# Second layer's value product turned round: activations stationary, value rows moving, sums kept in PSUM over all blocks

## The chip, the core and the metric

The kernel runs on one core of a Trainium2 chip. The metric is the device time of one execution in microseconds (us). A change of about 0.5% (20 us) is what the measurement of this kernel can tell from none.

## The reference

Two layers of a backbone over 512 latent tokens (width 1024) with 256 context tokens. Each layer has a token mixer and then PEER, a retrieval over 16384 experts, of which each token picks 128 (8 heads, 16 each). The part that matters here:

```python
def peer(h, wq, keys, u_tab, v_tab):
    ...                                                  # scores, two top-k, softmax
    def run(args):
        xc, ec, gc = args                                # tokens, experts, gates
        a = jax.nn.gelu(jnp.einsum('tkd,td->tk', u_tab[ec], xc))
        return jnp.einsum('tk,tkd->td', a * gc, v_tab[ec])
...
        if last:
            xl = xl + g2 * peer(hl, peer_wq[i], peer_keys[i], peer_u[i], peer_v[i])
...
    return rmsnorm(xl, final_g)
```

## The kernel before

**Layout.** The latent stream `x_l` stands feature-major: 128 partitions by 8 feature blocks by 512 tokens. Matrix products run in two parts: each fp32 operand is split into a rounded `hi` and a rest `lo` (float32r), and three matmuls (hi hi, hi lo, lo hi) make one product. `load_split` (lines 158 to 165) loads 512 KB of weights on SP's queue into a raw buffer, ACT rounds it (`whi`, L163), VectorE subtracts (`wlo`, L164).

**PEER in the second layer** (`peer`, from line 807). 384 of the 512 tokens (`TD`, three token tiles, `td`) are computed densely over all 128 blocks of 128 experts: an up-projection per block (`u_phase`, L822 to L829, matmuls in `proj` at L315 to L317, gelu by ACT at L825), a multiply with the dense gates `gt` (L999), a split into `ahi` and `alo` (L1004, L1005), and the value product. The last 128 tokens are gathered: GpSimd fetches the 128 rows of u and then of v that each token picked (L834, 512 KB each), and VectorE takes the dot products (`u_job`, L839) and the weighted sum (`v_job`, L850). At the end of `v_job` the sum is transposed back and added to `x_l` (L858, L862).

**Stages.** 62 of the 128 up-projections (`AHEAD`) are done early, while gates are being built, and spilled to HBM (`ad`); 66 are done inside the value stage (`prep` calls `u_phase`). All loads, and the gathered rows too, share one ring of nine raw buffers (`raw_tile`, 6 + 3). `pace` hands out the remaining gather jobs over the value stage: two steps for each up-projection, one for each value load.

**The value stage** (L1014 to L1034). It runs over 16 groups of eight expert blocks (`GS`). At a group's head all eight blocks are prepared (two of them already at the end of the group before, `EXC`); then, for each of the eight feature blocks `db`, one load of value weights, 24 matmuls with the value weights stationary and 384 tokens moving (L1020 to L1022), summed over the group's blocks in a PSUM tile `sc`, and one VectorE update of `x_l` from it (L1023). After the last group come the sums of squares (`stat`), `rsqrt`, a broadcast over TensorE (L252), eight scalings (L1042) and eight output transfers.

**Order.** The Tile framework orders each engine's instructions by a simulated timeline and generates the waits; each engine works through its list in order. PSUM has three tags with two buffers each: `mm` (one bank each), `sc` (two banks each) and `tp` (one bank each), eight banks in all.

## Time and profile before

| | us |
|---|---|
| median of 3 runs | 4072.15 (4067.31 to 4084.64) |
| profiled execution, its own time | 4055.16 |
| its span in the trace | 4053.4 |
| mean granted clock of TensorE over the span | 0.955 of 2.4 GHz |

The profile is that of one execution. Lines such as L1023 are lines of the kernel before. PE is TensorE, PEld its weight loads, DVE VectorE, ACT ScalarE, POOL GpSimd, SP the engine that issues most loads; SPq is its queue. PE's busy time includes the end of each matmul, which the next one overlaps, so starts are the better measure.

### The profile page before, as it was taken

How to read it: one execution, taken by the hardware profiler on the slowest of the kernel's cores; microseconds unless marked ns; L12 is line 12 of the kernel's file. 1: busy time of each engine (PE TensorE's matmuls, PEld its weight loads, DVE VectorE, ACT ScalarE, POOL GpSimd, SP SyncE). 2: the span in 40 equal slices, each digit the busy share in tenths (PEclk: the TensorE clock that was granted, in tenths of full speed). 3: DMA queues.
4: the chain of work that ended last, by engine and by line, in shares of the span. 5: the costliest groups of instructions: out<-in, count | busy, mean ns of one | idle time of the engine just before them, and what ended most of it. 6: DMA issues, size and time to landing. Idle time of an engine off the chain costs nothing. (4 is left out here: it accounts for less than half of the span.)

```text
span 4053.4 us, 54311 instructions
## 1 busy us (share of the span) xinstructions
PE 3695.2 (91%) x19469; PEld 3153.8 (78%) x19469; DVE 3273.7 (81%) x6850; ACT 1482.4 (37%) x2113; POOL 1050.3 (26%) x783
## 2 busy tenths in 40 slices
PE   7989889999978898999989988989999999998988
PEld 4777768877866777777768767779998888888887
DVE  8955799998997787788979885479998777777776
ACT  4344433224663222222322334433485332332322
POOL 0000000243324443455545300000003333333331
PEclk9989889999989999999999998999999999999998
DMA  7601135588989998999989662034579988888974
GB/s 247 224 31 44 52 111 168 185 311 301 338 308 315 309 315 295 316 327 327 334 303 339 235 226 79 1 120 130 164 283 340 313 291 284 281 280 278 310 267 157
DMA packets 378136, 966.64 MB, mean 238 GB/s; under 512 B 30712, under 2 KB 160552, under 8 KB 370312
## 3 DMA queue, kind: packets, MB, share of 16 engines
q1 hardware_dynamic: 239480, 467.60, 34.5%
q0 software_dynamic: 111312, 406.29, 29.2%
q10 hardware_dynamic: 27072, 89.27, 5.6%
q8 instruction: 153, 2.51, 0.2%
q14 instruction: 119, 0.97, 0.1%
HBM read 871.68 MB, written 91.36 MB: 238 GB/s over the span
## 5 line engine op out<-in xcount | busy, mean ns | idle before, releaser
L163 ACT ACTIVATE whi<-raw 128x1024 fp32r<-128x1024 f32 x640 | 672.6, 1057 | 1524.0 <-PE sc L1021 651.0
L834 POOL DMA_INDIRECT raw<-in_u_n_dram,E x384 | 499.3, 1300 | 2287.8 <-DVE wlo L164 1049.7
L315 PE MATMUL mm<-hi_l,whi 128*128 128x512 f32 (+1 forms) x2656 | 995.7, 375 | 18.7 <-ACT a L825 8.6
L317 PE MATMUL mm<-hi_l,wlo 128*128 128x512 f32 (+1 forms) x2656 | 989.0, 372 | 10.6 <-DVE wlo L164 10.6
L316 PE MATMUL mm<-lo_l,whi 128*128 128x512 f32 (+1 forms) x2656 | 990.3, 373 | 4.5 <-DVE lo_l L295 4.3
L1020 PE MATMUL sc<-ahi,whi 128*128 128x512 f32 (+1 forms) x2048 | 752.7, 374 | 82.7 <-DVE x_l L1023 69.3
L164 DVE TENSOR_TENSOR wlo<-raw,whi 128x1024 fp32r<-128x1024 f32 x640 | 776.4, 1217 | 62.3 <-ACT whi L163 54.2
L1021 PE MATMUL sc<-alo,whi 128*128 128x512 f32 (+1 forms) x2048 | 768.3, 376 | 60.4 <-DVE alo L1005 59.2
L1022 PE MATMUL sc<-ahi,wlo 128*128 128x512 f32 (+1 forms) x2048 | 760.3, 372 | 15.3 <-DVE wlo L164 15.2
L834 POOL DMA_INDIRECT raw<-in_v_n_dram,E x384 | 544.7, 1419 | 641.7 <-DVE ht L850 326.3
L839 DVE SCALAR_TENSOR_TENSOR raw<-raw,ht 128x1024 f32<-128x1024 f32 x384 | 466.6, 1221 | 170.9 <-DMA raw<-in_u_n_dram,E 169.3
L850 DVE SCALAR_TENSOR_TENSOR ht<-raw,wg,ht 128x1024 f32<-128x1024 f32 x381 | 487.8, 1280 | 129.9 <-DMA raw<-in_v_n_dram,E 127.5
L315 PEld LDWEIGHTS mm<-hi_l,whi 128*128 128x128 f32 x2656 | 502.9, 189 | 90.1 <-ACT a L825 11.1
L317 PEld LDWEIGHTS mm<-hi_l,wlo 128*128 128x128 f32 x2656 | 502.6, 189 | 81.1 <-DVE wlo L164 17.8
L316 PEld LDWEIGHTS mm<-lo_l,whi 128*128 128x128 f32 x2656 | 503.3, 189 | 73.9 <-DVE lo_l L295 9.2
L1020 PEld LDWEIGHTS sc<-ahi,whi 128*128 128x128 f32 x2048 | 395.6, 194 | 146.4 <-DVE x_l L1023 51.0
L1021 PEld LDWEIGHTS sc<-alo,whi 128*128 128x128 f32 x2048 | 397.9, 194 | 127.2 <-DVE alo L1005 87.6
L1022 PEld LDWEIGHTS sc<-ahi,wlo 128*128 128x128 f32 x2048 | 398.3, 194 | 59.4 <-DVE wlo L164 19.2
L1004 ACT ACTIVATE ahi<-a 128x512 fp32r<-128x512 f32 (+1 forms) x256 | 146.2, 577 | 543.9 <-DVE a L999 540.1
L958 ACT ACTIVATE gs<-sc 128x1024 f32<-128x1024 f32 x112 | 213.9, 2017 | 64.7 <-PE sc L956 61.0
L999 DVE TENSOR_TENSOR a<-a,gt 128x512 f32<-128x512 f32 (+1 forms) x256 | 156.1, 619 | 88.6 <-DMA gt<-gd 64.5
L1023 DVE SCALAR_TENSOR_TENSOR x_l<-sc,mods,x_l 128x512 f32<-128x512 f32 (+1 forms) x256 | 171.6, 679 | 68.0 <-PE sc L1022 65.8
(287 smaller groups left out, 3782.0 us busy)
## 6 DMA issues: line engine op xcount, KB each, us to landing
raw<-in_u_t_dram SPq DMA_DIRECT2D x256, 512.0 KB
raw<-in_v_b_dram SPq DMA_DIRECT2D x256, 512.0 KB
gd<-gs ACTq DMA_DIRECT2D x56, 1024.0 KB
raw<-in_w_adt_dram SPq DMA_DIRECT2D x64, 512.0 KB
gt<-gd SPq DMA_DIRECT2D x15, 2048.0 KB
raw<-in_wq_dram SPq DMA_DIRECT2D x48, 512.0 KB
gt<-gd SPq DMA_DIRECT2D x15, 1536.0 KB
ad<-a ACTq DMA_DIRECT2D x70, 256.0 KB
```

What stands on the lines that cost most here:

```text
L163: nc.scalar.activation(hi, raw, AF.Copy)
L164: nc.vector.tensor_tensor(lo, raw, hi.bitcast(F32), op=ALU.subtract)
L315: nc.tensor.matmul(ps, whi[:, k], hhi[:, k], start=(k == 0), stop=False)
L316: nc.tensor.matmul(ps, whi[:, k], hlo[:, k], start=False, stop=False)
L317: nc.tensor.matmul(ps, wlo[:, k], hhi[:, k], start=False, stop=(k == K - 1))
L834: nc.gpsimd.indirect_dma_start(out=g, out_offset=None, in_=tab, in_offset=bass.IndirectOffsetOnAxis(ap=G["E"][:, it, k:k + 1], axis=0), el ...
L839: nc.vector.scalar_tensor_tensor(g, g, 1.0, G["ht", it], op0=ALU.mult, op1=ALU.mult, accum_out=G["dots", it][:, k:k + 1])
L850: nc.vector.scalar_tensor_tensor(G["acc", it], g, G["wg", it][:, k:k + 1], G["acc", it], op0=ALU.mult, op1=ALU.add)
L958: nc.scalar.activation(gs[:, :, t8:t8 + 8].rearrange("p i t -> p t i"), ps, AF.Copy, scale=1.0 / WSC)
L1020: nc.tensor.matmul(ps, vh[:, c], wh, start=(c == 0), stop=False)
L1021: nc.tensor.matmul(ps, vh[:, c], wl, start=False, stop=False)
L1022: nc.tensor.matmul(ps, vl[:, c], wh, start=False, stop=(c == GS - 1))
```

## The change

In the second layer alone (`last`), the value product is turned round. For each expert block the activations of a token tile (128 experts by 128 tokens, `ahi` and `alo`) are stationary, and 128 natural value rows (128 experts by 1024 features, in two halves of 512) move: 18 matmuls of 512 columns for a block. The token-major sums of the three token tiles stay in six PSUM banks (both `sc` and both `tp` buffers) over all 128 blocks. Blocks are prepared two ahead instead of a group at a time, and the gates of a group (`gt`) are loaded one group ahead into a second buffer. A new `fin_setup` transposes `x_l` to token-major (`xt`) and spreads the gate `g2` over partitions at the head of the stage; a new `fin` adds gate times sum, norms and writes a token tile, for the gathered tile when its last row has come, for the three others after the last block. The final block after the two layers goes. The output and `final_g` are laid out token-major by the host code.

```diff
-    fg = const("final_g", [P, K])
...
             jobs = []
+            tok = {}
+
...
-                if k == P - 1:
+                if k == P - 1 and last:
+                    tok["fin"](td + it, [G["acc", it]])
+                elif k == P - 1:
                     xd, ms, ct = G["dst", it]
...
+            def fin_setup(pools):
+                fp = pools.enter_context(tc.tile_pool(name=nm("fin"), bufs=1))
+                xt = fp.tile([P, NL, D], F32, name=nm("x_tok"))
+                g2 = fp.tile([P, D], F32, name=nm("g2row"))
+                for hf in range(2):
+                    sl = slice(hf * 512, (hf + 1) * 512)
+                    pb = ps_mm()
+                    for k in range(4):
+                        nc.tensor.matmul(pb[:, k * P:(k + 1) * P], mcol(l, G2, 4 * hf + k, 0).to_broadcast([P, P]), ident,
+                                         start=True, stop=True)
+                    nc.scalar.activation(g2[:, sl], pb, AF.Copy)
+                for t in range(NL):
+                    for hf in range(2):
+                        pb = ps_mm()
+                        for k in range(4):
+                            nc.tensor.transpose(pb[:, k * P:(k + 1) * P], x_l[:, 4 * hf + k, t * P:(t + 1) * P], ident)
+                        nc.scalar.activation(xt[:, t, hf * 512:(hf + 1) * 512], pb, AF.Copy)
+
+                def fin(t, parts):
+                    w = D // len(parts)
+                    y = T(fp, [P, D], F32, "y", bufs=1)
+                    for j, ps in enumerate(parts):
+                        sl = slice(j * w, (j + 1) * w)
+                        nc.vector.tensor_tensor(y[:, sl], ps, g2[:, sl], op=ALU.mult)
+                        nc.vector.tensor_tensor(xt[:, t, sl], xt[:, t, sl], y[:, sl], op=ALU.add)
+                    ss = T(tiny, [P, 1], F32, "f_ss")
+                    nc.scalar.activation(y, xt[:, t], AF.Square, accum_out=ss)
+                    rstd = T(tiny, [P, 1], F32, "f_rs")
+                    rsqrt(rstd, ss, 1.0 / D, 1)
+                    nc.vector.scalar_tensor_tensor(xt[:, t], xt[:, t], rstd, fgr, op0=ALU.mult, op1=ALU.mult)
+                    nc.sync.dma_start(out[:, t], xt[:, t])
+
+                fgr = fp.tile([P, D], F32, name=nm("fgr"))
+                nc.sync.dma_start(fgr, a["final_g"])
+                tok["fin"] = fin
+
...
-                vps = [es2.enter_context(tc.tile_pool(name=nm("vp"), bufs=4))]
+                vps = [] if last else [es2.enter_context(tc.tile_pool(name=nm("vp"), bufs=4))]
...
-                vps.insert(0, es2.enter_context(tc.tile_pool(name=nm("vp"), bufs=6)))
+                vps.insert(0, es2.enter_context(tc.tile_pool(name=nm("vp"), bufs=4 if last else 6)))
+                gtps = [gtp]
+                if last:
+                    gtps.append(es2.enter_context(tc.tile_pool(name=nm("gtq"), bufs=1)))
+                    fin_setup(es2)
...
+                gts = {0: gt}
+
+                def load_gt(g):
+                    if 0 < g < ng and g not in gts:
+                        gts[g] = gt_tile(gtps[g % len(gtps)])
+                        nc.sync.dma_start(gts[g], gv[:, :TD // GT, g * GS:(g + 1) * GS, :])
 
                 def prep(g, c):
-                    nonlocal gt
-                    if g and c == 0:
-                        gt = gt_tile()
-                        nc.sync.dma_start(gt[:, :TD // GT], gv[:, :TD // GT, g * GS:(g + 1) * GS, :])
+                    load_gt(g)
+                    if last and c == 1:
+                        load_gt(g + 1)
+                    gt = gts[g]
...
-                for g in range(ng):
+                if last:
+                    halves = [slice(0, 512), slice(512, D)]
+                    acc2 = [ps_sc(), ps_sc()]
+                    accs = [[x[:, h] for h in halves] for x in acc2] + [[ps_tp(), ps_tp()]]
+                    prep(0, 0)
+                    prep(0, 1)
+                    for i in range(NKEYS):
+                        if i + 2 < NKEYS:
+                            prep(*divmod(i + 2, GS))
+                        wh, wl = ready.pop(divmod(i, GS))
+                        vh, vl = load_split(a["v_n"][e0 + i * P:e0 + (i + 1) * P], (P, D))
+                        for t in range(td):
+                            sl = slice(t * P, (t + 1) * P)
+                            for j, (w, v) in enumerate(((wh, vh), (wh, vl), (wl, vh))):
+                                for h in range(2):
+                                    nc.tensor.matmul(accs[t][h], w[:, sl], v[:, halves[h]], start=(i == 0 and j == 0),
+                                                     stop=(i == NKEYS - 1 and j == 2))
+                            if i == NKEYS - 1:
+                                tok["fin"](t, accs[t])
+                        pace(1)
+
+                for g in range(0 if last else ng):
...
-    o = T(hpool, [P, K, L], F32, "hi_l")
-    rb = rows(st_l)
-    for k in range(K):
-        nc.vector.scalar_tensor_tensor(o[:, k], x_l[:, k], fg[:, k:k + 1], rb, op0=ALU.mult, op1=ALU.mult)
-        nc.sync.dma_start(out[:, k], o[:, k])
```

## Rows read from the trace of the kernel before

**Rows 1.** The page: busy time of two engines (share of the span, instructions), and what the transfers moved in each of 40 equal slices of the span.

```profile
PE 3695.2 (91%) x19469; PEld 3153.8 (78%) x19469; DVE 3273.7 (81%) x6850; ACT 1482.4 (37%) x2113; POOL 1050.3 (26%) x783
...
GB/s 247 224 31 44 52 111 168 185 311 301 338 308 315 309 315 295 316 327 327 334 303 339 235 226 79 1 120 130 164 283 340 313 291 284 281 280 278 310 267 157
```

**Rows 2.** Two stretches, the value stage of the second layer and that of the first: length, then busy us of PE, PEld, DVE, ACT and POOL (instructions), granted clock, busy share of the DMA engines, GB/s.

```profile
3122.00:4037.00 915.00, 831.76 (x4498) 805.95 (x4498) 694.71 (x934) 278.00 (x382) 299.89 (x237) 0.95 0.83 277
1238.00:2342.00 1104.00, 1027.61 (x4391) 826.99 (x4390) 914.34 (x1118) 297.60 (x383) 526.55 (x377) 0.98 0.88 307
```

**Rows 3.** Timeline of TensorE in the second layer's value stage, 384 columns moving: start, us, what. 26 matmuls lie between the two.

```profile
4012.07 0.33 PE L1020 MATMUL sc<-ahi,whi 128*128 128x384 f32 x1
...
4016.75 0.33 PE L1020 MATMUL sc<-ahi,whi 128*128 128x384 f32 x1
```

**Rows 4.** The same in the first layer's value stage, 512 columns moving. 22 matmuls lie between the two.

```profile
2200.54 0.39 PE L1020 MATMUL sc<-ahi,whi 128*128 128x512 f32 x1
...
2205.75 0.39 PE L1022 MATMUL sc<-ahi,wlo 128*128 128x512 f32 x1
```

**Rows 5.** Groups of instructions in 3122 to 4037 us: line, engine, operation, tiles, shapes, count, busy us, mean ns of one, idle us before them and what ended it. L1020 to L1022 are alike, and L315 to L317.

```profile
L1021 PE MATMUL sc<-alo,whi 128*128 128x384 f32 x1008 | 354.1, 352 | 33.2 <-DVE alo L1005 33.2
L164 DVE TENSOR_TENSOR wlo<-raw,whi 128x1024 fp32r<-128x1024 f32 x186 | 225.3, 1218 | 7.5 <-ACT whi L163 6.7 <-issue 0.3 <-DMA raw<-in_v_b_dram 0.3
L163 ACT ACTIVATE whi<-raw 128x1024 fp32r<-128x1024 f32 x185 | 193.6, 1056 | 392.6 <-PE sc L1021 275.1 <-PE mm L316 64.5 <-issue 23.5
L315 PE MATMUL mm<-hi_l,whi 128*128 128x384 f32 x488 | 163.9, 336 | 1.7 <-ACT a L825 1.7
L850 DVE SCALAR_TENSOR_TENSOR ht<-raw,wg,ht 128x1024 f32<-128x1024 f32 x127 | 162.6, 1281 | 85.3 <-DMA raw<-in_v_n_dram,E 84.7
L839 DVE SCALAR_TENSOR_TENSOR raw<-raw,ht 128x1024 f32<-128x1024 f32 x109 | 133.1, 1223 | 72.4 <-DMA raw<-in_u_n_dram,E 72.2
L1023 DVE SCALAR_TENSOR_TENSOR x_l<-sc,mods,x_l 128x384 f32<-128x384 f32 x128 | 77.4, 613 | 33.8 <-PE sc L1022 31.8 <-issue 1.0
L999 DVE TENSOR_TENSOR a<-a,gt 128x384 f32<-128x384 f32 x120 | 64.9, 552 | 15.8 <-DMA gt<-gd 13.1 <-DMA a<-ad 2.6
L1005 DVE TENSOR_TENSOR alo<-a,ahi 128x384 fp32r<-128x384 f32 x120 | 64.3, 552 | 3.1 <-ACT ahi L1004 2.4
L858 PE MATMUL tp<-c_ident,ht 128*128 128x128 f32 x8 | 1.2, 272 | 0.0
```

**Rows 6.** Who waited for whom in 3122 to 4037 us: us in total, times, longest.

```profile
DVE ht L850 <- DMA raw<-in_v_n_dram,E: 84.7, 36, 5.7
DVE raw L839 <- DMA raw<-in_u_n_dram,E: 72.2, 55, 3.8
PE sc L1021 <- DVE alo L1005: 33.2, 25, 4.0
PE sc L1020 <- DVE x_l L1023: 27.0, 18, 5.3
PE sc L1022 <- DVE wlo L164: 15.2, 7, 3.6
DVE a L999 <- DMA gt<-gd: 13.1, 5, 4.5
```

**Rows 7.** Timeline at the head of one group, TensorE and VectorE: start, us, what, and in brackets the idle time before it and what ended it.

```profile
3405.76 1.23 DVE L839 SCALAR_TENSOR_TENSOR raw<-raw,ht 128x1024 f32<-128x1024 f32 x1 [3.12 <-DMA raw<-in_u_n_dram,E]
...
3406.91 1.49 DVE L1005 TENSOR_TENSOR alo<-a,ahi 128x384 fp32r<-128x384 f32 x3
...
3407.52 0.69 PE L1021 MATMUL sc<-alo,whi 128*128 128x384 f32 x1 [3.97 <-DVE alo L1005]
```

**Rows 8.** What SP's queue waited for in 3122 to 4037 us.

```profile
SPq L160 <- DVE wlo L164: 265.5, 68, 11.5
SPq L160 <- DVE raw L839: 157.0, 45, 7.3
```

**Rows 9.** Line L1020 in the first layer's value stage: TensorE's idle time before it by what ended it (us, times).

```profile
  DVE x_l L1023: 42.3, 23
```

**Rows 10.** Lines L825 and L427 over the whole span: count, duration in ns (least, median, most), first and last start, shapes.

```profile
L825 ACT ACTIVATE a<-mm x256: 461/528/618, 605.6 to 4005.3; 128x512 f32<-128x512 f32 x64, 128x384 f32<-128x384 f32 x64
...
L427 DVE TENSOR_TENSOR pp<-tp,sin x10: 681/684/692, 83.9 to 2421.0; 128x512 f32<-128x512 f32 x10
```

**Rows 11.** The end: the last matmul as the chain that ended last has it, then the timeline of VectorE (start, us, what).

```profile
4036.73 0.19 PE sc L1022
...
4039.74 0.16 DVE L239 TENSOR_SCALAR rq_v<-tp 128x3 f32<-128x3 f32 x1 [0.97 <-PE tp L267]
...
4041.91 0.16 DVE L247 SCALAR_TENSOR_TENSOR rstd_l<-rq_t,rq_y 128x3 f32<-128x3 f32 x1
...
4044.25 5.36 DVE L1042 SCALAR_TENSOR_TENSOR hi_l<-x_l,c_final_g,mm 128x512 f32<-128x512 f32 x8 [2.17 <-PE mm L252]
```

More of the change, by code (lines that the diff above doesn't have):

```diff
@@ L863, in v_job @@
                                                            op0=ALU.mult, op1=ALU.add)
-                    st = st_l if last else st_c
                     acc = T(cur["st"], [P, L], F32, "a")[:, :P]
                     for kk in range(K):
-                        stat(st, acc, kk, slice(ct * P, (ct + 1) * P),
+                        stat(st_c, acc, kk, slice(ct * P, (ct + 1) * P),
                              lambda: T(cur["st"], [P, L], F32, "a")[:, :P])
-                    stat_end(st, acc, ct, 1)
+                    stat_end(st_c, acc, ct, 1)
             for it in range(ng_):
@@ L893, in upto, with gt_tile @@
                 tick(nt - done[0])
+            def fin_setup(pools):
[31 more added lines that the diff above has]
+                tok["fin"] = fin
             gtp = es.enter_context(tc.tile_pool(name=nm("gtp"), bufs=1))
-            def gt_tile():
-                return T(gtp, [P, L // GT, GS, GT], F32, "gt", bufs=1)
+            def gt_tile(pool=None):
+                return T(pool or gtp, [P, TD // GT, GS, GT], F32, "gt", bufs=1)
             gt = gt_tile()
@@ L998, in prep @@
                     v3 = A.rearrange("p (b t) -> p b t", t=GT)
-                    nc.vector.tensor_tensor(v3, v3, gt[:, :TD // GT, c, :], op=ALU.mult)
-                    vp = vps[nv[0] % 10 // 6]
+                    nc.vector.tensor_tensor(v3, v3, gt[:, :, c, :], op=ALU.mult)
+                    vp = vps[0] if last else vps[nv[0] % 10 // 6]
                     nv[0] += 1
-                    hi = T(vp, [P, L], F32R, "ahi")[:, :TD]
-                    lo = T(vp, [P, L], F32R, "alo")[:, :TD]
+                    hi = T(vp, [P, TD], F32R, "ahi")
+                    lo = T(vp, [P, TD], F32R, "alo")
                     nc.scalar.activation(hi, A, AF.Copy)
@@ L1117, in _layout @@
                                 _cols(n["b_ada"])], axis=2)
-    r["final_g"] = n["final_g"].reshape(K, P).T
+    r["final_g"] = np.broadcast_to(n["final_g"], (P, D))
     r["sgu_w"] = n["sgu_w"].transpose(0, 3, 1, 2)
@@ L1136 @@
         args[name] = nc.dram_tensor(f"in_{name}_dram", arr.shape, mybir.dt.from_np(arr.dtype), kind="ExternalInput").ap()
-    args["out"] = nc.dram_tensor("out_0_dram", (P, K, L), F32, kind="ExternalOutput").ap()
+    args["out"] = nc.dram_tensor("out_0_dram", (P, NL, D), F32, kind="ExternalOutput").ap()
     with _tile.TileContext(nc, schedule_with_timeline_sim=True) as tc:
@@ L1141 @@
     o = np.asarray(r.results[0]["out_0_dram"])
-    return np.ascontiguousarray(o.transpose(2, 1, 0).reshape(1, L, D))
+    return np.ascontiguousarray(o.transpose(1, 0, 2).reshape(1, L, D))
```

## The prediction

> **What bounds the kernel now.** I read the page's engine table and slices first [rows 1]. TensorE is called busy 91% of the span, but that number includes the drain of each matmul, so it hides stalls; the reader should take from it only that VectorE, at 81%, is the second engine, and that the transfers run between 250 and 340 GB/s wherever the expert stages run. The change sits in one stage, so next I cut that stage out: from the first to the last eviction of the second layer's value product, 3122 to 4037 us, and beside it the same stage of the first layer, 1238 to 2342 us, which the change leaves alone [rows 2].
>
> What can the stage cost at least? Matmuls with 384 moving columns start 0.1733 us apart when nothing holds them (27 starts in 4.68 us) [rows 3], those with 512 columns 0.2265 us apart (23 starts in 5.21 us) [rows 4]. So a matmul costs its columns at 2.4 GHz (160 and 213 ns) plus about 13 ns, whatever its width. The window holds 3 x 1008 value matmuls and 3 x 488 up-projection matmuls (L315 to L317), all 384 wide [rows 5]: 4488 x 0.1733 = 778 us. It lasts 915 us. TensorE therefore loses 137 us there, 17.6% over its floor. In the first layer 4391 matmuls, taken all as 512 wide, make 995 us of 1104: 109 us lost, 11%.
>
> Where are the 137 us? The waits of TensorE [rows 6] name 33.2 us for `alo` (L1005), 27.0 us for the eviction `x_l` (L1023) that frees `sc`, 15.2 us for `wlo` (L164): 75 us. The rest is small waits and matmuls at the slow clock: the granted clock is 0.95 in the window [rows 2], that is, a tenth of the time at 1.2 instead of 2.4 GHz, after the stalls. All three releasers are VectorE, yet VectorE is busy only 695 of 915 us. The timeline of one group boundary shows how that fits [rows 7]: TensorE waits 3.97 us for an `alo`, while VectorE itself stands 3.12 us at a gathered row that has not landed (L839) and only then runs three `alo` in a row. VectorE works in order; at the head of a group of eight blocks it has to do the preparations (multiply L999, split L1005), the splits for the up-projections that belong to them and two gather jobs for each of those, all in one burst, while TensorE runs out of work. Over the window VectorE waits 84.7 + 72.2 us for gathered rows and 13.1 us for `gt` [rows 6]. SP in turn stands at ring slots for most of the window, 265.5 us of it until a VectorE split frees one [rows 8]: the nine raw buffers are always full.
>
> **The change part by part.**
>
> Matmuls. For each block 24 matmuls of 384 columns become 18 of 512: the columns stay, a quarter of the instructions go. In the window 3024 x 0.1733 = 524.1 us become 2268 x 0.2265 = 513.7: -10.4 us, for which TensorE's floor is 767 us. The rows of the two widths show a charge of 13 ns on each matmul that doesn't shrink with width [rows 3, 4]. The Trainium skill (TensorE: Matmul & The Clock Gate, section Back-to-back issue gap) gives the isolated warm gap as columns over 2.4 plus 2.5 ns; by that this term would be an estimated 2 us, and the trace, with 13 ns, disagrees.
>
> Evictions. 128 `x_l` updates of 0.613 us, 77.4 us of VectorE [rows 5], go, and with them the 27.0 us in which TensorE waited for one. Nothing replaces them before the end: the sums stay in six PSUM banks. What remains for other work is the pair of `mm` banks that the up-projection uses today; its wait for ACT's eviction (L825) is 1.7 us in 915 [rows 5], so I charge nothing. The Trainium skill (PSUM — Partial Sum Buffer, section Summary: rules for kernel authors) asks to evacuate promptly since PSUM is tight, which speaks against holding six banks; by the row the pressure could cost those 1.7 us.
>
> Preparation. Instead of bursts at the head of a group, each block's weights are made two blocks ahead, and `gt` one group ahead (the 13.1 us). The weights' buffers fall from ten to four, of which three are alive at once, so that costs nothing unless TensorE falls behind. Per pair of blocks, one of them with an up-projection, TensorE has 36 x 0.2265 + 24 x 0.1733 = 12.3 us [rows 3, 4]. VectorE has three splits (3 x 1.218), four preparation steps (4 x 0.552) and, with 237 gathers in the window, about 3.7 gather jobs of 1.25 us: 10.5 us, where it had 11.7 with evictions [rows 2, 5]. So VectorE has less to do than TensorE in every pair, not only on average over a group; the burst goes. What stays is its wait for gathered rows. Its busy time becomes 695 - 77 = 617 us; with all of today's 170 us of waiting that is 787 us.
>
> Transfers. The bytes are the same: the value rows come as 512 KB loads with 4 KB per partition either way, and 277 GB/s x 915 us = 253 MB [rows 2]. The best slices of 101 us move 339 to 341 GB/s [rows 1], so the transfers need at least 746 us. Three floors then, TensorE 767, VectorE with its waits 787, transfers 746, lie close together, behind a ring of nine buffers; the stage won't sit on any of them.
>
> How far above? The first layer's stage is the nearest row: it too has TensorE (995) beside transfers (307 GB/s x 1104 = 339 MB, 997 us at 340) and runs 11% over. Of its 109 us, 42.3 are waits for the eviction [rows 9], which the new stage can't have; without them it is 67 us, 6.7%. Upper and lower bound: 767 x 1.11 = 851 and 767 x 1.067 = 818 us. I take the middle, 836, since the bursts go too but the second layer gathers more per matmul. Against 915: -79 us (-64 to -97).
>
> Setup. `fin_setup` adds 40 matmuls of the kind of L858 (0.15 us each, eight in 1.2 us) [rows 5] and ten ACT copies of 128x512 (L825, at most 0.62 at that width) [rows 10]; with two `mm` buffers the copies set the pace, 10 x 0.6 = 6 us, of which up-projections can cover some or all. I take +4 (0 to 6). `final_g` comes as 512 KB on SP instead of 4 KB on POOL: 1.5 us at 340 GB/s, under the stage's first loads, at most +1.5 if not.
>
> Tail. Today 16.7 us pass from the last matmul (4036.73) to the end: eviction, statistics, `rsqrt`, broadcast, eight scaled outputs until 4049.6, the last transfer 3.8 us [rows 11]. Now each of three token tiles runs `fin`: four VectorE steps of 128x512 (0.68 each, L427) [rows 10], ACT's Square of 128x1024 (1.06, as L163) [rows 5], the `rsqrt` steps, 2.3 us from 4039.74 to 4042.07 [rows 11], and a scale of 1.28 (as L850): 6.3 us of VectorE each, 19 in all. The first begins 2.7 us before the last matmul (12 x 0.2265); `y` has one buffer, so the first Square is a wait of about 1.2 us, and the last transfer, 512 KB where it was 256, takes 3.8 + 0.8 us. The outputs' issues fall from eight to four on SP, which has nothing else left. 19 + 1.2 + 4.6 - 2.7 = 22 us: +6 (0 to 10). The gathered tile's own `fin` takes the place of its transposes and updates, some 6 us of VectorE within its slack, and at most +6 without it.
>
> Sum: -79 + 4 + 6 = -69 us. The profiled execution took 4055.16 us (span 4053.4, 1.8 us around it), so 3986; the median of the runs shown is 4072.15, 0.42% above the profiled one, so **4003 us**, -1.7%.
>
> **The rivals.**
>
> A, TensorE alone sets the stage. With the bursts gone the gathers land in time and nearly all 137 us come back: 767 us plus at most 25, so -123 to -148, with setup and tail -113 to -138: 3934 to 3959. For it: the pair count above, 12.3 against 10.5. Against it: the transfers would have to run at 253/780 = 324 GB/s throughout, which the first layer's stage (307) doesn't reach. The Trainium skill (DMA: Bandwidth & Descriptors, section Specifications) puts the fabric's ceiling at 435 GB/s, by which transfers would be no bound; no slice here passes 341. 0.17.
>
> B, the gathers keep the stage where it is. VectorE still stands at every late row, nine buffers still hold up SP and POOL, and the time that TensorE no longer loses at evictions it loses at `alo` and `wlo` instead: only the 10.4 us and a part of the 27.0 come back, and setup and tail take 10: 0 to -25, 4047 to 4072. For it: the chain that SP's waits show [rows 8], slots freed by VectorE. Against it: these waits lie at group heads. 0.14.
>
> C, two blocks ahead are too few. Today a group, once prepared, gives TensorE 192 x 0.1733 = 33 us without a new weight; now every block needs one, and the cover is 36 x 0.2265 = 8.2 us. A late gathered row plus a split and two preparations ahead of it pass that, and each time TensorE stops. It decides at a mean stop of (137 + 10 - 10)/128 = 1.07 us per block; at 1.3 us the kernel is 30 us slower, about 4100. Today's named 75 us are 0.6 us per block. 0.07.
>
> **How the numbers follow.** Forecast (-35 to -100 net, 3972 to 4037): 0.62, A 0.17, B 0.14, C 0.07. About 0.5%, 20 us, is what a measurement of this kernel can tell from no change: 4052 to 4092 counts as the same. Faster takes the forecast, A and a fifth of B: 0.82; same most of B: 0.11; slower C: 0.07. The range takes in most of A and half of B, leaving out about 0.05 below and 0.14 above: 3942 to 4060.
>
> **What would show it.** Right: 2304 value matmuls 0.2265 us apart, no wait for `x_l`, TensorE's waits for `alo` without a period of some 57 us, a granted clock of 0.97 or more, 295 to 315 GB/s, a stage of 818 to 851 us, 20 to 24 us after the last matmul. Wrong in size: a GB/s figure above 320 (A), or VectorE's waits for gathered rows growing past 250 us (B). Wrong in sign: TensorE's waits for `alo` spread over the blocks and above 137 us (C).

## The result and the profile after

The changed kernel takes 3903.22 us (median; 3900.21 to 3906.68), 0.9575 [0.9551, 0.9599] of the kernel before: 4.2% faster, where I forecast 4003 us. The profiled execution took 3904.18 us, 151 us less than that of before. One more execution of the kernel before took 14223.65 us and is left out of every comparison.

The page (engines; transfers in 40 slices):

```profile
PE 3644.7 (93%) x18725; PEld 3038.8 (78%) x18725; DVE 3208.8 (82%) x6734; ACT 1493.1 (38%) x2115; POOL 1064.6 (27%) x782
...
GB/s 249 224 48 45 43 97 157 152 299 289 338 348 277 320 332 313 320 318 335 332 329 323 339 173 251 22 1 141 130 174 285 321 344 341 343 348 337 345 343 187
```

The engine shares hardly move against [rows 1]. The last full slices do: 337 to 348 GB/s where the stage of before moved 267 to 313. The stage itself, from the first to the last value matmul, in the columns of [rows 2]:

```profile
3088.00:3884.00 796.00, 795.97 (x3839) 702.16 (x3840) 648.75 (x829) 289.11 (x385) 314.01 (x244) 1.00 0.92 328
```

796 us long, TensorE busy in all of it, the granted clock 1.00 throughout (0.95 before). Groups in that stretch, beside [rows 5] (line L1073 is the new value product, L316 an up-projection, L835 the gathers' issue):

```profile
L163 DVE TENSOR_TENSOR wlo<-raw,whi 128x1024 fp32r<-128x1024 f32 x192 | 235.2, 1225 | 118.1 <-ACT whi L162 117.0 <-issue 0.3
...
L316 PE MATMUL mm<-hi_l,wlo 128*128 128x384 f32 x512 | 171.8, 336 | 0.0
...
L1073 PE MATMUL sc<-whi,ahi 128*128 128x512 f32 x512 | 158.9, 393 | 4.7 <-ACT whi L162 4.7
L1073 PE MATMUL sc<-whi,alo 128*128 128x512 f32 x512 | 156.9, 392 | 0.0
```

The idle time in front of TensorE's groups is gone: what [rows 6] showed as 33.2, 27.0 and 15.2 us reads 0.0, but for 4.7 us in front of the stage's first matmul. Who still waits (3120 to 3880 us; total, times, longest):

```profile
ACT whi L162 <- PE tp L1073: 216.5, 109, 6.3
...
DVE wlo L163 <- ACT whi L162: 112.6, 111, 2.9
...
DVE raw L840 <- DMA raw<-in_u_n_dram,E: 4.8, 8, 1.3
...
DVE ht L851 <- DMA raw<-in_v_n_dram,E: 0.6, 2, 0.4
```

VectorE's waits for gathered rows fell from 156.9 us [rows 6] to 5.4. Everyone now waits for TensorE: ACT for a weight buffer that a value matmul still holds, VectorE for ACT behind it. That is the picture of a stage that one engine, TensorE, sets.

To measure "lost" the same way in every kernel, I take the stage from its first to its last value matmul, less its matmul starts at 0.1733 us (384 columns) and 0.2265 us (512) [rows 3, 4]:

| | stage us | matmul starts us | lost us |
|---|---|---|---|
| before | 929.3 | 792.0 | 137 |
| after | 796.4 | 788.0 (1536 of 384, 2304 of 512) | 8 |

Each loss here and below is that of one profiled execution. The seven further kernels that keep the second layer of after (e5, e6, e9, e15 to e18) lose 5 to 8 us in it; before was profiled once.

So of the 151 us between the two profiles 133 lie in this stage. Some 20 lie ahead of it, in the first layer's value stage (1104 and 1084 us), where TensorE, ACT and VectorE run the same instructions in the same order in both kernels. With that order it took 1092 to 1117 us in the eight profiles of before and its variants (mean 1100) and 1083 to 1098 in six of after and its variants (mean 1089). So about half of the 20 us seems to go with the kernel and the rest is scatter; why this unchanged stage is shorter in the kernels made from after is open. The tail costs 1.5 more. The medians differ by some 20 us more than the profiles: the executions of before scatter over 42 us (4057 to 4099 over all runs), those of after over 15 (3897 to 3912, e6 among them), and the profiled one of before (4055) was shorter than all of these. Where its longer ones lose was not profiled.

### The profile page after: what moved, and what is told of

Same layout as the page of the kernel before. It is cut to its first block, busy times and chain, and to the rows that moved or that the text cites. A ratio compares the mean times of both kernels' runs of the same rounds, so it can differ in the third digit from the quotient of the medians.

```text
span 3902.4 us, 52533 instructions
## 1 busy us (share of the span) xinstructions
PE 3644.7 (93%) x18725; PEld 3038.8 (78%) x18725; DVE 3208.8 (82%) x6734; ACT 1493.1 (38%) x2115; POOL 1064.6 (27%) x782
## 4 chain that ended last, share of the span: by engine, by line
PE 41%; issue 10%; DMA 7%; DVE 6%; POOL 5%; ACT 2%; ACTq 0%; POOLq 0%; SPq 0%; DVEq 0%
PE sc L1073 9%; PE mm L314 6%; PE mm L315 6%; PE mm L316 6%; POOL raw L835 5%; PE tp L1073 4%; DMA raw<-in_v_n_dram,E 2%; PE sc L1089 2%; PE sc L1090 2%; PE sc L1091 2%; DVE ht L851 1%; DMA gt<-gd 1%; DVE wlo L163 1%; PE mm L592 1%; DMA raw<-in_u_n_dram,E 1%
## 5 line engine op out<-in xcount | busy, mean ns | idle before, releaser
L835 POOL DMA_INDIRECT raw<-in_u_n_dram,E x384 | 511.2, 1331 | 2226.2 <-DVE wlo L163 1031.4
L314 PE MATMUL mm<-hi_l,whi 128*128 128x512 f32 (+1 forms) x2656 | 995.9, 375 | 11.8 <-ACT whi L162 5.7
L316 PE MATMUL mm<-hi_l,wlo 128*128 128x512 f32 (+1 forms) x2656 | 988.9, 372 | 7.6 <-DVE wlo L163 7.5
L315 PE MATMUL mm<-lo_l,whi 128*128 128x512 f32 (+1 forms) x2656 | 990.7, 373 | 4.5 <-DVE lo_l L294 4.3
L835 POOL DMA_INDIRECT raw<-in_v_n_dram,E x384 | 547.7, 1426 | 545.8 <-DVE ht L851 268.6
L316 PEld LDWEIGHTS mm<-hi_l,wlo 128*128 128x128 f32 x2656 | 502.2, 189 | 78.0 <-DVE wlo L163 13.5
L315 PEld LDWEIGHTS mm<-lo_l,whi 128*128 128x128 f32 x2656 | 502.9, 189 | 76.9 <-DVE lo_l L294 9.3
L1089 PE MATMUL sc<-ahi,whi 128*128 128x512 f32 x1024 | 399.7, 398 | 34.2 <-DVE x_l L1092 30.5
L1090 PE MATMUL sc<-alo,whi 128*128 128x512 f32 x1024 | 407.4, 399 | 24.4 <-DVE alo L1053 23.6
L1091 PE MATMUL sc<-ahi,wlo 128*128 128x512 f32 x1024 | 404.1, 395 | 0.9 <-DVE wlo L163 0.9
L1089 PEld LDWEIGHTS sc<-ahi,whi 128*128 128x128 f32 x1024 | 194.3, 190 | 87.1 <-DVE x_l L1092 23.5
L1090 PEld LDWEIGHTS sc<-alo,whi 128*128 128x128 f32 x1024 | 195.5, 191 | 77.5 <-DVE alo L1053 38.4
L1091 PEld LDWEIGHTS sc<-ahi,wlo 128*128 128x128 f32 x1024 | 195.6, 191 | 41.7 <-DVE wlo L163 1.8
L1053 DVE TENSOR_TENSOR alo<-a,ahi 128x512 fp32r<-128x512 f32 (+1 forms) x256 | 157.5, 622 | 11.7 <-ACT ahi L1052 11.3
```

Of the source, the lines that this page charges most:

```text
L314: nc.tensor.matmul(ps, whi[:, k], hhi[:, k], start=(k == 0), stop=False)
L315: nc.tensor.matmul(ps, whi[:, k], hlo[:, k], start=False, stop=False)
L316: nc.tensor.matmul(ps, wlo[:, k], hhi[:, k], start=False, stop=(k == K - 1))
L835: nc.gpsimd.indirect_dma_start(out=g, out_offset=None, in_=tab, in_offset=bass.IndirectOffsetOnAxis(ap=G["E"][:, it, k:k + 1], axis=0), el ...
L1089: nc.tensor.matmul(ps, vh[:, c], wh, start=(c == 0), stop=False)
L1090: nc.tensor.matmul(ps, vh[:, c], wl, start=False, stop=False)
```

## Experiments

Two theories at first, to explain why 129 of the 137 lost us came back where I had 68. **Theory 1**: the bursts of preparations at group heads cost it, whatever the product. **Theory 2**: the evictions and their hold on `sc`. Later **theory 3**: the old product needs all eight blocks' weights before it can finish any feature block, so a burst leaves TensorE with nothing, while the new one works on each weight as it comes. **Theory 4**: bursts only hurt because VectorE's ordered queue also holds the gather jobs. Ratios are to executions of before taken beside each kernel.

**e1: before, preparations spread.** One block of the next group is prepared after each feature block; sixteen weight buffers instead of ten. The second layer's weight and gate tiles are also cut to its 384 tokens.

```diff
-EXC = [..., {6: (0,), 7: (1,)}]
+EXC = [..., {db: (db,) for db in range(8)}]
...
-                vps.insert(0, ...(name=nm("vp"), bufs=6))
+                vps.insert(0, ...(name=nm("vp"), bufs=16 if last else 6))
```

> The kernel before with one edit: in the second layer the eight preparations of the next group are spread over the eight feature blocks of the running group (one after each), with 16 weight buffers; product, evictions and group sums stay as they were. Theory 1 (the 137 us that TensorE lost in the stage came from the preparation bursts at the group heads): 90 to 130 us faster than before, the value stage from 930 us down to 800 to 840, TensorE's waits for alo near zero, though 128 evictions are still there. Theory 2 (they came from the evictions, VectorE's 77 us and the wait for a free sc bank): at most 40 us faster, stage 890 us or more, waits for x_l as before.

3941.25 us, 0.9676 [0.9638, 0.9714]. The stage, then its waits:

```profile
3112.00:3918.00 806.00, 795.23 (x4545) 789.22 (x4543) 693.66 (x948) 283.41 (x389) 331.21 (x237) 1.00 0.91 319
```

```profile
PE sc L1022 <- DVE wlo L164: 5.5, 5, 2.4
...
PE sc L1020 <- DVE x_l L1023: 2.5, 4, 1.3
...
DVE raw L839 <- DMA raw<-in_u_n_dram,E: 9.7, 12, 1.8
...
DVE ht L850 <- DMA raw<-in_v_n_dram,E: 9.4, 12, 2.3
```

Lost 19 us instead of 137, with the old product, its 128 evictions and VectorE as busy as before (694 us). The waits for gathered rows go with the bursts: they were not the gathers' own latency. So most of the gain is to be had without turning the product round.

**e2: before without evictions.** The second layer's sums are added to `x_l` for the last group alone.

```diff
+                        if not last or g == ng - 1:
                             nc.vector.scalar_tensor_tensor(x_l[:, db, :TD], ps, ...)
```

> The kernel before with the second layer's evictions of groups 0 to 14 left out (the sums of those 15 groups are missing from the output); preparation bursts stay. Theory 1 (bursts): 20 to 50 us faster than before, the waits for alo at group heads remain at 25 us or more. Theory 2 (evictions): 90 to 130 us faster, stage near 810 us.

4044.29 us, 0.9922 [0.9888, 0.9956]; lost 126. TensorE's waits in the stage:

```profile
PE sc L1021 <- DVE alo L1005: 39.4, 29, 5.6
PE sc L1022 <- DVE wlo L164: 13.4, 10, 3.6
PE sc L1020 <- ACT whi L163: 9.2, 7, 2.7
...
PE sc L1020 <- DVE x_l L1024: 0.3, 1, 0.3
```

The 27.0 us for `x_l` [rows 6] went. Between the two profiles 11 us of lost time came back, and TensorE's waits for `alo` and `whi` grew: it arrived earlier at weights that were late anyway. The medians differ by 32 us (18 to 46 by the interval), so what the evictions cost lies somewhere from 11 to 46 us. Theory 2, which asked for 90 to 130, falls either way.

**e3: after with the bursts put back.** Preparations at group heads as before, one `gt`, eight weight buffers; the product stays turned round.

```diff
+                        if c == 0:
+                            for c_ in range(GS):
+                                if (g, c_) not in ready:
+                                    prep(g, c_)
-                        if i + 2 < NKEYS:
-                            prep(*divmod(i + 2, GS))
```

> The changed kernel with the preparation put back to what it was: all eight blocks of a group at its head (two of them at the end of the group before), one gt buffer, eight weight buffers; product turned round, sums in PSUM, no evictions. Theory 1 (bursts): 70 to 120 us slower than the changed kernel, stage 870 to 915 us instead of 797. Theory 2 (evictions): within 30 us of the changed kernel, since the evictions are still gone.

3903.57 us, 0.9573 [0.9537, 0.9609], the time of after; lost 5.

```profile
3113.00:3892.00 779.00, 777.37 (x3765) 685.79 (x3764) 631.25 (x809) 277.24 (x374) 325.58 (x240) 1.00 0.92 331
```

My expectation of 70 to 120 us slower fell, and theory 1 in its simple form with it. A burst, a single `gt` (17.9 us of waits on VectorE) and late rows (27.3 us for `raw` alone) all pass without stopping TensorE. So it is neither the burst nor the old product by itself, but the two together: theory 3.

The traces show why. One group head of before, then one of e3, each with the group's first value matmul and its last `alo`:

```profile
3389.87 0.33 PE L1020 MATMUL sc<-ahi,whi 128*128 128x384 f32 x1
...
3409.93 0.55 DVE L1005 TENSOR_TENSOR alo<-a,ahi 128x384 fp32r<-128x384 f32 x1
```

```profile
3406.93 1.09 PE L1071 MATMUL sc<-whi,ahi 128*128 128x512 f32 x4
...
3426.70 0.55 DVE L1050 TENSOR_TENSOR alo<-a,ahi 128x384 fp32r<-128x384 f32 x1
```

The last of a group's eight weights is equally late in both: done 16.9 us after the group's first value matmul in before and 16.7 in e3 (medians of 15 groups, counted in the traces; 12.3 to 20.6 and 13.0 to 20.6). In these stretches TensorE stands idle for 51 us in all in before and not at all in e3. The old product needs that weight in its first pass of 24 matmuls (4.2 us), the new one only at the eighth block.

**e4, e13, e14: before, half the need.** If theory 3 holds, the first two feature blocks of a group computed together, block by block, should let TensorE start on each weight. e4 does that; the pair holds two of the three split buffers, so e13 gives the second layer four split buffers, and e14 is the control with four split buffers and no pairing.

```diff
+                        if PAIR[l] and db == 0:          # e4, e13
+                            vs = [load_split(a["v_b"][l, g, q], (P, GS, P)) for q in range(2)]
+                            pb = ps_sc([P, 2, 512])
+                            for c in range(GS):
+                                for q, (vh, vl) in enumerate(vs):
+                                    ...                  # three matmuls into pb[:, q, :TD]
...
-            cur["wb"] = WB
+            cur["wb"] = WB + int(last)                   # e13, e14
```

> The kernel before with one edit in the second layer: the first two feature blocks of each group are computed together, block by block (for each expert block six matmuls, three into each half of one sc tile), so that the eight weights of a group are needed over 8.3 us instead of 4.2; bursts, evictions and group sums stay. Theory 3, formed after e3_burst (TensorE stops because the product needs all eight fresh weights within one pass of 24 matmuls; the burst alone doesn't hurt): the lost time of the stage falls from 137 us by some 16 x 4 us to 60 to 100, 40 to 80 us faster than before. Rival (the turned-round product is immune for another reason: wider matmuls, fewer weight loads, no evictions): within 20 us of before.

> e4_pair with four split buffers instead of three in the second layer, since in e4_pair the pair held two of the three and TensorE's waits moved from alo to the splits. If that was the reason why e4_pair gained nothing: the waits for wlo and whi go too and 30 to 80 us come back against before. If VectorE's backlog at the group head stops TensorE at whatever comes next: within 25 us of before.

> The kernel before with four split buffers in the second layer and nothing else: the control for e13_pair4. Within 20 us of before by every theory, unless the three buffers hold up the splits at the group heads, which would show as 30 us or more.

| | us | ratio | lost us |
|---|---|---|---|
| e4 | 4090.08 | 1.0047 [1.0026, 1.0069] | 175 |
| e13 | 4047.22 | 0.9933 [0.9914, 0.9952] | 116 |
| e14 | 4110.18 | 1.0085 [1.0064, 1.0107] | 205 |

TensorE's waits of e4, then of e13, then of e14:

```profile
PE sc L1035 <- DVE x_l L1038: 51.6, 17, 7.4
PE sc L1027 <- DVE wlo L165: 28.4, 13, 8.5
...
PE sc L1026 <- DVE alo L1006: 4.3, 5, 1.8
```

```profile
PE sc L1035 <- DVE x_l L1038: 45.6, 20, 8.2
PE sc L1026 <- DVE alo L1006: 23.6, 23, 4.1
PE sc L1027 <- DVE wlo L165: 7.6, 4, 4.9
```

```profile
PE sc L1021 <- DVE alo L1005: 53.8, 36, 3.7
PE sc L1020 <- DVE x_l L1023: 50.5, 17, 9.3
PE sc L1020 <- ACT ahi L1004: 14.7, 8, 4.1
```

In e4 the pairing takes the wait for `alo` away (33.2 to 4.3) and the time is lost at `wlo` and `x_l` instead. With four split buffers (e13) the wait for `wlo` falls to 7.6, but that for `x_l` stays at 45.6 and that for `alo` is back at 23.6, so a shortage of split buffers was only part of it. Against its own control e13 gives back 89 us of lost time, 63 us between the medians. But the control is worse than before, by 68 us lost and 38 us of median: more split buffers hurt. I read that as splits running ahead of preparations in VectorE's queue; that is argued, not shown. Against before itself e13 gains 25 us, between its two forecasts (30 to 80, and within 25). So halving the need did not bring the gain that theory 3 forecast; the theory rests on e3 beside e2 and on the group heads above.

**e12: before without the second layer's gather jobs.** No rows are fetched for the last 128 tokens.

```diff
+            if last:
+                done[0] = len(jobs)
```

> The kernel before without any gather job in the second layer (the last 128 tokens get no expert sum; their statistics are taken from the stream as it stands): 256 transfers of 512 KB, 126 MB of the stage's 253, and some 310 us of VectorE leave the stage; preparation bursts, the product and the evictions stay. Theory 4 (VectorE or the transfers are overrun at the group head): the lost time falls from 137 us to under 40, the stage to 800 to 830 us. Theory 3 (the chain from the last up-projection over four steps to a pass that needs all eight weights stops TensorE by itself): at least 80 us stay lost, stage 870 us or more.

3919.73 us, 0.963 [0.961, 0.9649]; lost 11. The stage, and the one wait of TensorE that is left (at its weight loads, PEld):

```profile
3108.00:3901.00 793.00, 786.50 (x4511) 781.07 (x4509) 423.50 (x560) 281.53 (x374) 0.00 (x0) 1.00 0.54 163
```

```profile
PEld sc L1027 <- DVE x_l L1030: 10.9, 16, 0.7
```

Bursts, old product and evictions all stay, and TensorE loses only 0.7 us at each of 16 group heads. VectorE is busy 424 of 793 us and the transfers move half. The last weight of a group is done 8.9 us after its first value matmul, where before had 16.9. So theory 4 holds too, in this form: the need for all eight weights costs time only when gather jobs stretch the burst. By which way, e12 can't say: it takes away their work on VectorE, their waits for late rows, their share of the raw buffers and half of the transfers at once, and no run here parts these. In before the stretch from the third multiply of a group to its last `alo` holds five gather jobs on average, some 6 us of work, and 1.9 us of waits in front of them (counted in the trace).

**e7, e10, e11: how much slack after has.** e7 adds, in the program's text, one VectorE operation of 128x384 per block whose result nobody reads; e10 takes the early `gt` and its second buffer away; e11 prepares one block ahead instead of two.

```diff
+                        nc.vector.scalar_tensor_tensor(x_l[:, i % K, :TD], ...)   # e7
-                    if last and c == 1:                                            # e10
-                        load_gt(g + 1)
-                            prep(*divmod(i + 2, GS))                               # e11
+                            prep(*divmod(i + 1, GS))
```

> The changed kernel with one more VectorE step of 128x384 for each of the 128 blocks, multiply and add on x_l, which nothing reads any more: about 0.55 us each, 70 us in all, nearly what the evictions cost. If VectorE's load mattered in the new stage it gets 40 to 70 us slower. If TensorE alone sets it: within 10 us of the changed kernel.

> The changed kernel with one gt buffer and no early load of the next group's gates. If the early load is part of the gain, each of 15 groups waits for a transfer of 1.5 MB (4 to 8 us) that two blocks of cover (8 to 16 us) hide in part: 10 to 50 us slower. If the cover is enough, within 10 us.

> The changed kernel with weights prepared one block ahead instead of two, so that the cover is 4.1 us of value matmuls, 8.2 with an up-projection. By rival C of the prediction (blocks too few ahead) TensorE stops at many blocks: 30 to 130 us slower. If TensorE's order, in which matmuls of either kind fill in for each other, hides it: within 15 us.

| | us | ratio | lost us |
|---|---|---|---|
| e7 | 3948.08 | 0.9691 [0.9666, 0.9715] | 44 |
| e10 | 3931.91 | 0.9651 [0.9618, 0.9684] | 44 |
| e11 | 3934.03 | 0.9658 [0.9616, 0.9699] | 36 |

The stage of e7, its first 145 us, and where the added operations ran; then two waits of e10:

```profile
3105.00:3936.00 831.00, 807.03 (x3839) 703.46 (x3840) 702.74 (x937) 286.39 (x385) 325.69 (x244) 0.99 0.88 314
3105.00:3250.00 145.00, 122.99 (x534) 101.38 (x535) 144.60 (x241) 40.74 (x55) 45.91 (x35) 0.94 0.76 253
```

```profile
L1077 DVE SCALAR_TENSOR_TENSOR x_l<-x_l,mods x128: 601/607/635, 3090.5 to 3240.3; 128x384 f32<-128x384 f32 x128
```

```profile
DVE a L1044 <- DMA gt<-gd: 68.4, 15, 8.6
...
PE sc L1070 <- ACT ahi L1049: 22.8, 8, 4.9
```

Each is 30 to 46 us slower than after. But e7 is not the test that it was meant to be: nothing ties the added operations to their blocks, and all 128 (78 us) ran between 3090 and 3240 us, just before the stage and in its first 135 us, where VectorE was then busy nearly without a break (144.6 of 145 us). Some 36 of its 44 lost us lie there. So it shows what a VectorE without any free time does to the stage; how much more work VectorE could take when it is spread was not measured. With the block-wise preparation `gt` ahead and two blocks ahead are both needed. With e3's bursts, which prepare two to seven blocks ahead, the early `gt` was not.

**e8, e9: the gather jobs handed out otherwise** (PWU, steps per up-projection: none in the second layer of before; none in the first layer of after).

```diff
-PWU = [2, 2]
+PWU = [2, 0]      # e8, on before
+PWU = [0, 2]      # e9, on after
```

> The kernel before with one constant changed: in the second layer's value stage no gather jobs are tied to the up-projections any more, all go with the value loads (about 1.9 for each instead of 0.9), so the burst at a group head is some eight gather jobs of 1.25 us shorter; preparations, product and evictions stay. Theory 4 (TensorE stops because VectorE's ordered queue owes more work at the group head than TensorE has matmuls to run in that time, whichever instruction TensorE happens to stand at): half or more of the 137 us come back, 60 to 110 us faster. Rival (the product's need of all eight weights at once): within 25 us of before, since the eight preparations still come together.

> The changed kernel with the same constant in the first layer, whose stage still has group bursts. Theory 4: 30 to 70 us faster than the changed kernel, 3835 to 3875 us. Rival: within 15 us of it.

4081.42 us, 1.0023 [1.0008, 1.0038], and 3960.83, 0.9732 [0.9697, 0.9767]. In e8 the gather jobs between the third multiply and the last `alo` of a group did not become fewer (six on average, five in before, counted in the traces), so the edit did not make the change that was to be tested and says nothing on theory 4. In e9 they did not become fewer either (eight, seven in after); the first layer's stage grows to 1138 us, against both forecasts.

**e15: transfers.** One more load of 128 KB per block, into a tile that nobody reads.

> The changed kernel with one more load of 128 KB for each of the 128 blocks, which nothing reads: 16.8 MB, so that the stage needs 348 GB/s instead of 327 to hold its time. If the transfers have room (its best slices move 343 to 348): within 12 us of the changed kernel. If they are at their ceiling: 20 to 50 us slower.

3926.67 us, 0.9636 [0.9617, 0.9655], but all 128 loads ran long before the stage:

```profile
L1071 SPq DMA_DIRECT2D xtra<-in_v_n_dram x128: 327/328/422, 10.6 to 364.2; - x128
```

The stage kept its 795 us; the 25 us that e15 is slower than e6 lie ahead of the first layer's value stage, which begins at 1270 us instead of 1239. What the extra bytes would do in the stage was not measured.

**e5, e6, e16 to e18: the first layer.** e6 is after once more (3901.74 us, 0.9584 [0.9556, 0.9611]). Its first-layer value stage still loses about 90 us (the 1104 us of before against 995 [rows 2, 4] were 109). e5 puts e4's pairing there; e16 to e18 prepare three, four and four of eight blocks ahead there instead of two, as far as memory allows, paid for with one stash tile (e16), one stash tile and one raw buffer (e17), or three stash tiles (e18).

```diff
-EXC = [{6: (0,), 7: (1,)}, ...]
+EXC = [{5: (0,), 6: (1,), 7: (2,)}, ...]              # e16; eleven weight buffers
+EXC = [{4: (0,), 5: (1,), 6: (2,), 7: (3,)}, ...]     # e17, e18; twelve
```

> The changed kernel with the same edit of e4_pair in the first layer, whose value product is still feature-major with bursts: its stage loses about 90 to 110 us over its floor. Theory 3: 20 to 50 us of it come back, 3855 to 3885 us. Rival: within 15 us of the changed kernel.

> The changed kernel once more, as control beside the other runs of this call: 3900 to 3910 us, its second value stage 790 to 800 us; the first layer's stage, whose instruction order is that of before, anywhere between 1080 and 1110 us.

> After, with one more block of the next group prepared ahead in the first layer (three of eight instead of two, EXC), eleven weight buffers instead of ten and four stash tiles instead of five. If the first layer's stage loses its time to the same bursts at group heads (the theory of the interaction), five preparations at the head instead of six give back a part: stage of 1065 to 1085 us where the kernels with the same order of the first layer show 1081 to 1117, 5 to 25 us faster in all. If its loss comes from transfers (the rival), no change beyond that scatter.

> After, with four of eight blocks of the next group prepared ahead in the first layer, twelve weight buffers, paid for with a ring of eight raw buffers there instead of nine and four stash tiles. Theory of the interaction: four preparations at the head instead of six, 10 to 40 us faster, unless the shorter ring takes it back. Rival (transfers): slower, by the missing raw buffer.

> After, with four of eight blocks of the next group prepared ahead in the first layer, twelve weight buffers, paid for with stash tiles alone (two instead of five), the ring of nine raw buffers kept. Theory of the interaction: 10 to 40 us faster, unless the two stash tiles make the preparations wait for one another. Rival (transfers): no change, or slower by that wait.

| | us | ratio | first layer's stage us |
|---|---|---|---|
| e6 (after) | 3901.74 | 0.9584 [0.9556, 0.9611] | 1087 |
| e5 | 3900.54 | 0.9586 [0.9562, 0.9609] | 1081 |
| e16 | 3918.08 | 0.9622 [0.9589, 0.9654] | 1099 |
| e17 | 3902.39 | 0.9572 [0.9542, 0.9603] | 1089 |
| e18 | 3993.98 | 0.9794 [0.9762, 0.9826] | 1176 |

In e18 the wait that grew is the one for `ahi`, which I read as preparations that lack a stash tile (TensorE, first-layer value product):

```profile
L1089 PE MATMUL sc<-ahi,whi 128*128 128x512 f32 x999 | 404.8, 412 | 80.0 <-ACT ahi L1052 45.3 <-DVE x_l L1092 33.4 <-ACT whi L162 1.2
```

None gains. e5 has the three split buffers with which e4 gained nothing. In e17 the last `alo` of a group is done 11.8 us after its first value matmul instead of 16.7 (medians, counted in the traces), and the stage is no shorter. But at least four of eight preparations still stand at the head, and each price may have eaten a gain, so this neither shows nor excludes that the first layer loses its time as the second did. That stays open. e17 shows that a ring of eight raw buffers there costs nothing that can be measured together with the spread. No kernel here beats after by more than its measurement can tell.

**The picture**, us lost in the second layer's stage:

| | all eight weights needed (old product) | block by block (new product) |
|---|---|---|
| burst at group heads | 137 (before), 126 without evictions (e2), 11 without gather jobs (e12) | 5 (e3) |
| spread | 19 (e1) | 8 (after) |

It is an interaction. Any one of three things removes nearly all of the loss: no burst, the product turned round, no gather jobs. Their savings must not be added.

## Why the prediction was wrong

**The step that failed** is "How far above?", the term of the stage: 836 us in its window, 9% over the floor, taken as the middle between 11% and 6.7% of the first layer's stage as "the nearest row". The stage came out 1% over: 8 us lost where the term had kept 69. The first layer's stage was no analogue. It has the same product that needs all eight weights and the same group heads, the very two things that the change takes away (whether its loss comes from them stays open, as said above). Only its eviction waits were subtracted, and in the second layer e2 got back 11 us of 137 for them in the profile. What the working had found a paragraph earlier, a burst meeting an ordered queue, should have priced the term: with burst and need gone, the stalls of 137 us had no place left to happen.

**The transfers' floor** held the forecast away from rival A: 324 GB/s "which the first layer's stage (307) doesn't reach". The stage ran at 328. That row showed what the stage had asked for, not what the transfers can give; and slices of 101 us average too much. Finer slices of the same trace of before (11 us, 800 to 1240 us) read:

```profile
GB/s 287 296 332 303 335 325 320 314 285 287 328 324 299 221 303 242 347 324 357 300 304 373 361 290 355 363 340 310 295 406 291 394 371 342 291 269 207 240 267 288
```

and those of after over its stage (20 us):

```profile
GB/s 292 310 395 325 332 346 332 380 308 344 354 333 359 342 314 339 338 395 308 314 377 317 361 320 339 386 295 355 373 317 364 314 354 328 331 378 333 310 165 37
```

So "no slice here passes 341" was true of the page's slices alone (their highest is 340). The Trainium skill (DMA: Bandwidth & Descriptors, section Specifications), whose 435 GB/s I set aside for that row, agrees with the finer ones: none passes it.

**Rival A is what happened.** TensorE alone sets the stage, with the sign that I had named for it, GB/s above 320. Its own sum, -113 to -138, holds what the change brought in the profile (-133 and +1.5); the rest of the 151 us lies in the first layer, and 3903 is below its 3934 because of that and of the median's distance to the profile. What spoke for it, 12.3 us of TensorE to 10.5 of VectorE per pair of blocks, was right: the chain that ended last shows one pair after the other at 12.39 us, and VectorE's 649 us over 64 pairs are 10.1.

```profile
3111.65 2.76 PE sc L1073 x12
3124.04 2.76 PE sc L1073 x12
3136.42 2.76 PE sc L1073 x12
```

**Evictions.** Right that no wait for `x_l` is left and that holding six banks costs nothing: no matmul of an up-projection waits for its bank. The rule of the Trainium skill that speaks against it (PSUM — Partial Sum Buffer, section Summary: rules for kernel authors) has no price here. What the 27.0 us were worth is less clear than I had it: e2 gives back 11 us in the profile and 32 in the median.

**Matmuls.** Right: 2304 of them, ten starts in 2.27 us at the end (3881.53 to 3883.80), 0.227 each.

```profile
3881.53 0.61 PE L1073 MATMUL sc<-whi,ahi 128*128 128x512 f32 x2
...
3883.80 0.61 PE L1073 MATMUL tp<-whi,alo 128*128 128x512 f32 x2
```

**Preparation.** Right that two blocks ahead suffice and that `gt` must come early (e10); the buffers cost nothing. My reason that the burst alone was the harm was half of it (e3).

**Setup**, +4 forecast: not to be seen. From the last matmul of the gates to the first value matmul 28.9 us pass, 31.4 before. What the chain that ended last shows in that gap is transfers:

```profile
3063.13 9.53 DMA gd<-gs
3073.17 13.73 DMA raw<-in_v_n_dram
```

The first value load sets the start; `fin_setup` lies beside it.

**Tail**, +6 forecast, +1.5 measured. VectorE and the last output's issue:

```profile
3882.34 0.68 DVE L920 TENSOR_TENSOR y<-sc,g2row 128x512 f32<-128x512 f32 x1
...
3885.44 0.15 DVE L238 TENSOR_SCALAR rq_v<-f_ss 128x1 f32<-128x1 f32 x1 [1.22 <-ACT y L923]
...
3897.18 1.29 DVE L926 SCALAR_TENSOR_TENSOR x_tok<-x_tok,f_rs,fgr 128x1024 f32<-128x1024 f32 x1
3898.49 0.33 SPq L927 DMA_DIRECT2D out_dram<-x_tok  x1
```

The Square's wait is the 1.2 us forecast. The three `fin` take 16.1 us, not 19: the `rsqrt` chains, charged at 2.3 us each, run between other tiles' steps and mostly pass inside them.

**Rivals B and C.** B fell: VectorE's waits for gathered rows shrank to 5 us. C fell as put, two blocks being enough, but e11 shows its mechanism at one block: 32 us against e6.

## What to carry to other kernels

When an engine of medium load stalls the bound one, look for a burst in its ordered queue and for a consumer that needs the whole burst before it can go on; removing either gives nearly all back, so price the pair and not the parts. A stage that shares the suspected cause is no measure for the stage without it: take its loss to pieces first, and start from the floor. A transfer rate seen in a stage that something else holds back is demand; read fine slices before calling it a ceiling.

## What the hardware showed that was not expected

One core moved 328 GB/s over 796 us, half of it gathered rows, with slices of 20 us up to 395, and once the value product had begun TensorE never waited. The clock followed the stalls: 0.95 granted with 137 us lost, 1.00 with 19 or fewer (before, e1, e12, e3, after), and 0.99 with 44 (e7), and of the 137 us of before only 103 are start intervals of over 0.6 us. Another 180 starts lie about twice the 0.1733 us apart, 176 of them in the 85 us at 1.2 GHz, and cost 26 us more (counted in the trace). A stall costs more than its own length.
